# Score products of the recurrent heads: the second head of each pair in the other half of TensorE's columns

## The chip, the cores and the metric

The kernel runs on one core of one Trainium2 chip. The metric is the device time of one execution in microseconds (us); runs of the same kernel are summed up by their median. A profile of one execution gives the span from its first to its last instruction, and that is a little shorter than the time of a run.

The engines are named as in the profile: PE is TensorE's matrix multiply, PEld its loading of the stationary operand ("weights", here also keys), DVE is VectorE, ACT is ScalarE, POOL is GpSimd and SP is SyncE. Matmuls write into PSUM; only PE writes there by multiplying, and ACT and DVE read from there. A PSUM tile here has 128 partitions of 512 float32 values.

## The reference, cut to what matters

The reference is a trunk of two layers over 512 frames of 1024 channels. Each layer has a feed-forward block, a mixing block, a cross-attention into 256 memory tokens and a second feed-forward block. The change is in the mixing block, in the part with four recurrent heads of 128 channels:

```python
proj = h @ w_in[l]
q_a, f_a, i_a, g_a, u_b = jnp.split(proj, splits, axis=-1)
...
log_f = jnp.logaddexp(jnp.log(lbh), jnp.log1p(-lbh) + jax.nn.log_sigmoid(z))
k = (1.0 - lbh) * jax.nn.sigmoid(-z)
...
b = jnp.cumsum(gc, axis=2)
o_inter = jnp.einsum('bhtk,bhkv->bhtv', qc * jnp.exp(b), S)
rel = b[:, :, :, None, :] - b[:, :, None, :, :]
decay = jnp.exp(jnp.where(causal, rel, -jnp.inf))
A = jnp.einsum('bhtk,bhsk,bhtsk->bhts', qc, kc, decay)
o = o_inter + jnp.einsum('bhts,bhsv->bhtv', A, vc)
```

So each head needs, in each stretch of frames, a triangle of scores A[t, s]: query t times key s, with every channel decayed by the product of the forget gates between s and t.

## The kernel before, in words

The frames lie along the free axis: a head's `q`, `f` (forget gate), `kg` (key) are 128 channels by 512 frames. Heads go in pairs: `g` is the pair (0 or 1), `hh` the head in it. The 512 frames are NT = 4 blocks of P = 128 frames, HT = 256 is half of the frames.

The kernel works the triangle of a 128-frame block out by levels, `levels()` in `mix` (L809): m = 1, 2, 4, ... 64. At level m the block is cut into pieces of 2m frames; queries of a piece's second half meet keys of its first half. Between levels, keys (`kg`, L849) and queries (`qf`, L850) are multiplied by the forget products `tot` of the half that lies between them, so no exponent is ever needed. All scores end in `atd`, one 128 by 128 tile (key by query) for every head and block, which is read as an operand at L974.

Level 1 is done by column sums. Levels 2 to 32 are `dense(g, m)` (L785). `first_halves` (L767) has gathered the keys of all first halves, 64 a block, into `keys`. For each head and block a float32 matmul multiplies 64 keys by 64 queries (L793): eight matmuls a pair, which write partitions 0 to 63 of one PSUM tile, one head in columns 0 to 255, the other in 256 to 511. Only small squares on the diagonal of each 64 by 64 result are wanted. At level 32 they are copied from PSUM to `atd` by four small ACT copies a pair (L798). At levels 2 to 16 ACT copies each pair's tile into one half of `packed` (L802), and after the second pair ACT issues DMAs that bring the rows of `packed` to the partitions of `spread` at which those keys stand in `atd` (L807): 2, 4, 8 and 4 DMAs at levels 2, 4, 8 and 16. One level later DVE copies them into `atd` under a mask (`place`, L763). Level 64 (L824 to L833) has its own matmuls (L831) and one ACT copy a pair (L832).

What sets the order: the levels are a generator that is stepped between other matrix products of the stage (gate columns, value rows, pooling columns) at places written out by hand, `STEPS`. Each engine runs its own instructions strictly in the order the program has for it, and a scheduler at build time may bring other ready work forward. Tiles of PSUM used here come from one pool of four, `ps_tile`. ACT's queue carries its copies, the casts of weights (`split`, L76: `whi`; DVE makes `wlo` at L77) and the issue of the `spread` DMAs, all in one order. Weights are split five blocks ahead of their use and loaded seven ahead, by SP's queue.

Of the kernel before, what the change touches and what calls it, by code (L numbers as in the profile page):

```python
# [7 lines left out]
F32 = mybir.dt.float32  # L8
# [6 lines left out]
P = 128  # L15
D = 1024
T = 512
# [3 lines left out]
NT = T // P  # L21
# [25 lines left out]
def trunk_kernel(ctx: ExitStack, tc: tile.TileContext, ap: dict, out: bass.AP):  # L47
    nc = tc.nc
    pe, act, dve, pool = nc.tensor, nc.scalar, nc.vector, nc.gpsimd
# [11 lines left out]
    def ps_tile():  # L61
        return pp.tile([P, 512], F32, tag="ps", name="ps")
# [5 lines left out]
    def s_tile(shape, dt, name):  # L68
        return sp.tile(shape, dt, tag="s", name=name)
# [401 lines left out]
    HT = T // 2  # L471
# [242 lines left out]
    def mix(l, norm, mem, after):  # L714
# [4 lines left out]
        atd = [s_tile([P, 2, NT, P], F32, "atd") for _ in range(2)]  # L719
# [3 lines left out]
        for h in range(H):  # L723
            ps = ps_tile()
# [12 lines left out]
        for h in range(H):  # L737
            ps = ps_tile()
# [6 lines left out]
        def products(a, b):  # L745

            t = tp.tile([P, T], F32, tag="sq", name="qk", bufs=4)
            hl = s_tile([P, 2, T], F32R, "qkp")
            pool.tensor_tensor(t if len(a.shape) == 2 else t.rearrange("p (h n) -> p h n", h=2), a, b, op=ALU.mult)
            split(hl[:, 0], hl[:, 1], t)  # L750
            return hl

        def column_sums(ps, hl):

            for c in range(2):
                pe.matmul(ps, ones_r, hl[:, c], start=c == 0, stop=c == 1)  # L756

        def place(g, m, rows):

            o = atd[g].rearrange("p h i (b e j) -> p (h i) b e j", e=2, j=m)[:, :, :, 1, :]  # L760
            src = rows.rearrange("p (x b j) -> p x b j", x=2 * NT, j=m)
            mk = masks[m].rearrange("p (o b j) -> p o b j", o=1, j=m).broadcast_to([P, 2 * NT, 64 // m, m])
            dve.copy_predicated(o, mk, src)  # L763

        keys = [None, None]

        def first_halves(g, m):  # L767


            keys[g] = tp.tile([P, T], F32, tag="sq", name="keys", bufs=4)  # L770
            src = kg[g].rearrange("p h (b e j) -> p h b e j", e=2, j=m)[:, :, :, 0, :]
            if m > 4:
                act.copy(keys[g].rearrange("p (h b j) -> p h b j", h=2, j=m), src)
                return
            for hh in range(2):
                dst = keys[g][:, hh * HT:(hh + 1) * HT].rearrange("p (i j b) -> p i b j", i=NT, j=m)
                act.copy(dst, src[:, hh].rearrange("p (i b) j -> p i b j", i=NT))
# [4 lines left out]
        spread = {m: spreads[i % 2] for i, m in enumerate((2, 4, 8, 16))}  # L782
        packed = [None]

        def dense(g, m):  # L785


            ps = ps_tile()
            for hh in range(2):
                for i in range(NT):  # L790
                    c = hh * HT + i * 64
                    b = qf[g][:, hh, i * P:(i + 1) * P].rearrange("p (b e j) -> p b e j", e=2, j=m)[:, :, 1, :]
                    pe.matmul(ps[0:64, c:c + 64], keys[g][:, c:c + 64], b, start=True, stop=True)  # L793
            if m == 32:
                for b in range(2):
                    src = ps[b * 32:b * 32 + 32].rearrange("p (h i t) -> p h i t", h=2, i=NT)[:, :, :, b * 32:b * 32 + 32]
                    for hh in range(2):
                        act.copy(atd[g][b * 64:b * 64 + 32, hh, :, b * 64 + 32:b * 64 + 64], src[:, hh])  # L798
                return
            if g == 0:  # L800
                packed[0] = s_tile([64, 2, T], F32, "packed")
            act.copy(packed[0][:, g], ps[0:64])  # L802
            if g == 1:
                n = max(m, 64 // m)
                for x in range(64 // n):
                    rows = slice(x, P, 2 * m) if m <= 4 else slice(2 * m * x, 2 * m * x + m)
                    nc.scalar.dma_start(spread[m][rows], packed[0][x * n:(x + 1) * n])  # L807

        def levels():  # L809

            tot = f
            odd = [qf[g].rearrange("p h (n e) -> p h n e", e=2)[:, :, :, 1] for g in range(2)]
            even = [kg[g].rearrange("p h (n e) -> p h n e", e=2)[:, :, :, 0] for g in range(2)]
            near = [[products(q[g][:, hh], kg[g][:, hh]) for hh in range(2)] + [products(odd[g], even[g])] for g in range(2)]
            yield
            for m in (1, 2, 4, 8, 16, 32, 64):
                nb = T // (2 * m)
                tots = [None, None]  # L820
                if 1 < m <= 32:
                    for g in range(2):
                        dense(g, m)
                elif m > 32:  # L824
                    for g in range(2):
                        ps = ps_tile()
                        for hh in range(2):
                            for i in range(NT):
                                a = kg[g][:, hh, i * P:i * P + 64]
                                b = qf[g][:, hh, i * P + 64:(i + 1) * P]  # L830
                                pe.matmul(ps[0:64, (hh * NT + i) * 64:(hh * NT + i + 1) * 64], a, b, start=True, stop=True)  # L831
                        act.copy(atd[g][0:64, :, :, 64:128].rearrange("p h i t -> p (h i) t"),  # L832
                                 ps[0:64, :].rearrange("p (x t) -> p x t", t=64))  # L833
                for g in range(2):
                    if m == 1:
                        for hh in range(2):
                            ps = ps_tile()
                            column_sums(ps, near[g][hh])
                            dve.tensor_tensor(atd[g][:, hh], ps.rearrange("p (i t) -> p i t", t=P),
                                              ident.rearrange("p (o t) -> p o t", o=1).broadcast_to([P, NT, P]), op=ALU.mult)  # L840
                            yield
                        ps = ps_tile()
                        column_sums(ps, near[g][2])
                        place(g, m, ps)
                    tv = tot[g].rearrange("p h (b e) -> p h b e", e=2)
                    kv = kg[g].rearrange("p h (b e j) -> p (h b) e j", e=2, j=m)
                    qv = qf[g].rearrange("p h (b e j) -> p (h b) e j", e=2, j=m)
                    tx = tot[g].rearrange("p h (b e) -> p (h b) e", e=2)
                    dve.tensor_tensor(kv[:, :, 0, :], kv[:, :, 0, :], tx[:, :, 1:2].broadcast_to([P, 2 * nb, m]), op=ALU.mult)  # L849
                    dve.tensor_tensor(qv[:, :, 1, :], qv[:, :, 1, :], tx[:, :, 0:1].broadcast_to([P, 2 * nb, m]), op=ALU.mult)  # L850
                    nt_ = s_tile([P, 2, nb], F32, "tot") if m == 1 else sm.tile([P, 2, nb], F32, tag=f"tot{m}", name="tot", bufs=2)
                    dve.tensor_tensor(nt_, tv[:, :, :, 0], tv[:, :, :, 1], op=ALU.mult)
                    tots[g] = nt_
                    if m < 32:
                        first_halves(g, 2 * m)
                    if m == 1:
                        yield
                if 2 < m <= 32:
                    for g in range(2):
                        place(g, m // 2, spread[m // 2][:, g])  # L860
                if m > 1:
                    yield
                tot = tots
            last.extend(tot)
# [26 lines left out]
        def recurrent():  # L891
            yield from levels()
            turn(0), turn(1), turn(2)
            yield
# [14 lines left out]
        for h in range(H):  # L909
            ps = ps_tile()  # L910
# [7 lines left out]
        for k2 in range(NK // 2):  # L918
            wh, wl = wts.next()
            for e in range(2):  # L920
                k = 2 * k2 + e
                for i in range(NT):
                    sl = slice(i * P, (i + 1) * P)
                    mm3(accs[i], (norm.h[k][0][:, sl], norm.h[k][1][:, sl]), (wh[:, e], wl[:, e]),
                        start=k == 0, stop=k == NK - 1)
# [6 lines left out]
        for g in POOL_ORDER:  # L932
            win = 2 ** (g + 1)
            ps = ps_tile()
# [5 lines left out]
            src, dst, w_ = u, sa, 1  # L940
            while w_ < win:
                pool.tensor_tensor(dst[:, 16:], src[:, 16:], src[:, 16 - w_:16 + T - w_], op=ALU.add)
                src, dst = dst, (sb if dst is sa else sa)
# [23 lines left out]
        o = [None] * H  # L967
# [328 lines left out]
```

## Time and profile before

| | |
|---|---|
| runs | 2098.34, 2098.62, 2100.18 us |
| median of 3 | 2098.62 us |
| span of the profiled execution | 2096.8 us |
| mean granted TensorE clock | 0.999 of full speed |
| recurrent-score stage, layer 0 | about 400 to 490 us after the start |
| the same, layer 1 | about 1440 to 1530 us |

How to read the lines that follow. A page opens with the busy time of each engine, its share of the span and its number of instructions. The chain of work is followed back from the last instruction, at each step to what released it. A line of a timeline has the start in us, the duration in us, engine, source line, operation, output tile, inputs, shapes and a count of merged instructions, then the engine's idle time before it and what ended that. The view of one source line or tile lists minimum, median and maximum duration in ns. Instructions that issue DMAs stand under the queue of their engine (ACTq is ACT's) and aren't counted as busy. Some tile names: `whi` and `wlo` are the two parts of a split weight block, `h` the normed input, `sg` the gates.

### The profile page before, as it was taken

What the parts mean: (1) busy time and instruction counts of PE and PEld (TensorE: products, weight loads), DVE (VectorE), ACT (ScalarE), POOL (GpSimd) and SP (SyncE); (2) the same over time, 40 slices, a digit from 0 to 9 for tenths busy, and PEclk for the clock granted to TensorE, in tenths of its full rate; (3) what the DMA queues carried; (4) which work ended last, traced back from release to release, by engine and by line L of the source; (5) the groups of instructions that cost most, each with busy time, mean ns of one, the idle gap of its engine ahead of it and who ended that gap; (6) DMA issues with size and microseconds to landing.
All of it is one profiled execution on the core that took longest, in us unless ns stands there. A gap on an engine that the chain in (4) does not pass through costs nothing.

```text
span 2096.8 us, 29543 instructions
## 1 busy us (share of the span) xinstructions
PE 2087.3 (100%) x11538; PEld 1809.1 (86%) x11538; DVE 1412.3 (67%) x2126; ACT 919.8 (44%) x1465; POOL 205.0 (10%) x204
## 2 busy tenths in 40 slices
PE   9999999999999999999999999999999999999998
PEld 8889898888888888989888898988888888889897
DVE  7758576677646585766776685757776556768575
ACT  6425344434544343544534353445344444435343
POOL 1100000302000110000021000003210001100000
PEclk9999999999999999999999999999999999999999
DMA  5364554233533246646425746532334331474552
GB/s 187 119 182 124 145 156 161 61 99 98 151 103 103 61 131 171 157 122 185 123 69 153 188 116 177 158 108 71 92 112 135 111 112 45 141 208 124 146 138 79
DMA packets 107868, 268.33 MB, mean 128 GB/s; under 512 B 10832, under 2 KB 12880, under 8 KB 107728
## 3 DMA queue, kind: packets, MB, share of 16 engines
q1 hardware_dynamic: 93952, 224.49, 32.9%
q0 software_dynamic: 11952, 38.02, 10.3%
q10 hardware_dynamic: 1824, 3.93, 0.8%
q8 instruction: 91, 1.49, 0.3%
q14 instruction: 49, 0.40, 0.1%
HBM read 256.70 MB, written 2.10 MB: 123 GB/s over the span
## 4 chain that ended last, share of the span: by engine, by line
PE 98%; DVE 1%; issue 1%; ACT 0%; POOL 0%; POOLq 0%; ACTq 0%; DVEq 0%
PE ps L86 19%; PE ps L84 19%; PE ps L85 19%; PE acc L554 8%; PE acc L84 8%; PE acc L85 8%; PE acc L86 8%; PE acc L555 4%; PE ps L1025 1%; PE ps L793 1%; PE ps L1026 1%; PE ps L974 0%; PE ps L1091 0%; PE acc L346 0%; PE ps L756 0%
## 5 line engine op out<-in xcount | busy, mean ns | idle before, releaser
L77 DVE TENSOR_TENSOR wlo<-raw,whi 128x1024 fp32r<-128x1024 f32 (+1 forms) x334 | 394.5, 1202 | 78.4 <-ACT whi L76 63.2
L76 ACT CAST whi<-raw 128x1024 fp32r<-128x1024 f32 (+1 forms) x334 | 330.3, 1018 | 113.1 <-DMA raw<-in_ffn_w_dram 49.9
L85 PE MATMUL ps<-h,whi 128*128 128x512 f32 x848 | 330.2, 390 | 0.0
L84 PE MATMUL ps<-h,whi 128*128 128x512 f32 x848 | 329.7, 391 | 0.0
L86 PE MATMUL ps<-h,wlo 128*128 128x512 f32 x848 | 329.5, 390 | 0.0
L554 PE MATMUL acc<-bhl,whi 128*128 128x512 f32 x744 | 266.3, 398 | 0.0
L86 PE MATMUL ps<-bhl,wlo 128*128 128x256 f32 x744 | 210.8, 284 | 0.2
L85 PE MATMUL ps<-bhl,whi 128*128 128x256 f32 x744 | 209.9, 283 | 0.0
L84 PE MATMUL ps<-bhl,whi 128*128 128x256 f32 x744 | 209.8, 283 | 0.0
L555 PE MATMUL acc<-bhl,wlo 128*128 128x256 f32 x744 | 204.8, 281 | 0.0
L76 ACT CAST whi<-wsum 128x1024 fp32r<-128x1024 f32 x124 | 130.1, 1050 | 151.8 <-DVE wsum L165 87.3
L86 PEld LDWEIGHTS ps<-h,wlo 128*128 128x128 f32 x848 | 159.2, 188 | 33.4
L84 PEld LDWEIGHTS ps<-h,whi 128*128 128x128 f32 x848 | 159.1, 188 | 33.1
L85 PEld LDWEIGHTS ps<-h,whi 128*128 128x128 f32 x848 | 159.2, 188 | 32.9
L77 DVE TENSOR_TENSOR wlo<-wsum,whi 128x1024 fp32r<-128x1024 f32 x124 | 153.8, 1240 | 47.7 <-ACT whi L76 45.5
L554 PEld LDWEIGHTS acc<-bhl,whi 128*128 128x128 f32 x744 | 137.7, 189 | 24.0
L84 PEld LDWEIGHTS ps<-bhl,whi 128*128 128x128 f32 x744 | 141.6, 190 | 4.1
L86 PEld LDWEIGHTS ps<-bhl,wlo 128*128 128x128 f32 x744 | 141.5, 190 | 2.5 <-DVE wlo L77 1.6
L555 PEld LDWEIGHTS acc<-bhl,wlo 128*128 128x128 f32 x744 | 141.1, 190 | 2.8
L85 PEld LDWEIGHTS ps<-bhl,whi 128*128 128x128 f32 x744 | 141.6, 190 | 1.9
L134 POOL DMA_DIRECT2D wsum<-in_ffn_w_dram x62 | 53.9, 869 | 765.5 <-DMA wsum<-in_ffn_w_dram 364.5
L84 PE MATMUL acc<-ahl,whi 128*128 128x512 f32 x328 | 128.0, 390 | 0.0
(271 smaller groups left out, 4128.9 us busy)
## 6 DMA issues: line engine op xcount, KB each, us to landing
raw<-in_ffn_w_dram SPq DMA_DIRECT2D x198, 512.0 KB
wsum<-in_ffn_w_dram SPq DMA_DIRECT2D x124, 256.0 KB
wsum<-in_ffn_w_dram POOLq DMA_DIRECT2D x62, 512.0 KB, 6.8
raw<-in_w_in_dram SPq DMA_DIRECT2D x32, 512.0 KB
raw<-in_ffn_w_dram SPq DMA_DIRECT2D x62, 256.0 KB
raw<-in_w_out_dram SPq DMA_DIRECT2D x16, 512.0 KB
raw<-in_xa_wk_dram SPq DMA_DIRECT2D x16, 512.0 KB
raw<-in_xa_wq_dram SPq DMA_DIRECT2D x16, 512.0 KB
```

The source lines that it names most:

```text
L76: act.copy(hi, src)
L77: dve.tensor_tensor(lo, src, hi.bitcast(F32), op=ALU.subtract)
L84: pe.matmul(o, a[0], b[0], start=start, stop=False, skip_group_check=more)
L85: pe.matmul(o, a[0], b[1], start=False, stop=False, skip_group_check=more)
L86: pe.matmul(o, a[1], b[0], start=False, stop=stop, skip_group_check=more)
L134: nc.gpsimd.dma_start(s1, c2, accum_op=ALU.add)
L554: pe.matmul(ps.rearrange("p (c t) -> p c t", t=HT), w[0], t, start=start and k == 0, stop=False, skip_group_check=True)
L555: pe.matmul(ps[:, :HT], w[1], t[:, 0], start=False, stop=k == 3, skip_group_check=True)
L793: pe.matmul(ps[0:64, c:c + 64], keys[g][:, c:c + 64], b, start=True, stop=True)
L1025: pe.matmul(ps.rearrange("p (c m) -> p c m", m=M), whl[0][:, k], mn[k], start=k == 0, stop=False, skip_group_check=True)
L1026: pe.matmul(ps[:, :M], whl[1][:, k], mn[k][:, 0], start=False, stop=k == NK - 1, skip_group_check=True)
```

## The change

At levels 2 to 64 the second head of each pair writes partitions 64 to 127 of the PSUM tile, where the first head writes 0 to 63, and the loops are turned so that the two heads alternate, block by block. Each head then needs 256 columns of the tile, so at levels 2 to 32 both pairs share one tile. At levels 2 to 16 one ACT copy of 128 by 512 takes the place of two of 64 by 512; the rows of the two heads are now apart, so each DMA to `spread` becomes two of half the bytes. At level 32 the four copies a pair stay, with other source places, and at level 64 one copy a pair becomes two of half the length. Nothing else is changed.

```diff
         def dense(g, m):
-            ps = ps_tile()
-            for hh in range(2):
-                for i in range(NT):
+            if g == 0:
+                packed[0] = ps_tile()
+            ps = packed[0]
+            for i in range(NT):
+                for hh in range(2):
                     c = hh * HT + i * 64
                     b = qf[g][:, hh, i * P:(i + 1) * P].rearrange("p (b e j) -> p b e j", e=2, j=m)[:, :, 1, :]
-                    pe.matmul(ps[0:64, c:c + 64], keys[g][:, c:c + 64], b, start=True, stop=True)
+                    o = g * HT + i * 64
+                    pe.matmul(ps[hh * 64:hh * 64 + 64, o:o + 64], keys[g][:, c:c + 64], b, start=True, stop=True)
             if m == 32:
-                for b in range(2):
-                    src = ps[b * 32:b * 32 + 32].rearrange("p (h i t) -> p h i t", h=2, i=NT)[:, :, :, b * 32:b * 32 + 32]
-                    for hh in range(2):
-                        act.copy(atd[g][b * 64:b * 64 + 32, hh, :, b * 64 + 32:b * 64 + 64], src[:, hh])
+                for hh in range(2):
+                    for b in range(2):
+                        src = ps[hh * 64 + b * 32:hh * 64 + b * 32 + 32, g * HT:(g + 1) * HT]
+                        src = src.rearrange("p (i t) -> p i t", i=NT)[:, :, b * 32:b * 32 + 32]
+                        act.copy(atd[g][b * 64:b * 64 + 32, hh, :, b * 64 + 32:b * 64 + 64], src)
                 return
-            if g == 0:
-                packed[0] = s_tile([64, 2, T], F32, "packed")
-            act.copy(packed[0][:, g], ps[0:64])
             if g == 1:
+                t = s_tile([P, 2, HT], F32, "packed")
+                act.copy(t.rearrange("p g t -> p (g t)"), ps)
                 n = max(m, 64 // m)
                 for x in range(64 // n):
                     rows = slice(x, P, 2 * m) if m <= 4 else slice(2 * m * x, 2 * m * x + m)
-                    nc.scalar.dma_start(spread[m][rows], packed[0][x * n:(x + 1) * n])
+                    for hh in range(2):
+                        nc.scalar.dma_start(spread[m][rows, :, hh * HT:(hh + 1) * HT], t[hh * 64 + x * n:hh * 64 + (x + 1) * n])
...
                     for g in range(2):
                         ps = ps_tile()
-                        for hh in range(2):
-                            for i in range(NT):
+                        for i in range(NT):
+                            for hh in range(2):
                                 a = kg[g][:, hh, i * P:i * P + 64]
                                 b = qf[g][:, hh, i * P + 64:(i + 1) * P]
-                                pe.matmul(ps[0:64, (hh * NT + i) * 64:(hh * NT + i + 1) * 64], a, b, start=True, stop=True)
-                        act.copy(atd[g][0:64, :, :, 64:128].rearrange("p h i t -> p (h i) t"),
-                                 ps[0:64, :].rearrange("p (x t) -> p x t", t=64))
+                                pe.matmul(ps[hh * 64:hh * 64 + 64, i * 64:(i + 1) * 64], a, b, start=True, stop=True)
+                        for hh in range(2):
+                            act.copy(atd[g][0:64, hh, :, 64:128], ps[hh * 64:hh * 64 + 64, :HT].rearrange("p (i t) -> p i t", t=64))
```

## The prediction

> **What bounds the kernel now.** I read the page first: span, busy shares, chain.
>
> ```profile
> span 2096.8 us, 29543 instructions
> PE 2087.3 (100%) x11538; PEld 1809.1 (86%) x11538; DVE 1412.3 (67%) x2126; ACT 919.8 (44%) x1465; POOL 205.0 (10%) x204
> PE 98%; DVE 1%; issue 1%; ACT 0%; POOL 0%; POOLq 0%; ACTq 0%; DVEq 0%
> ```
>
> PE works without a break and 98% of the chain is PE. A microsecond taken from PE's own work is therefore worth a microsecond, as long as the next PE instruction finds its operands ready. ACT, at 44%, has room on average, but averages say nothing of the stage that is edited. So next come the instructions of the edited line (level 2 to 32 scores), and the timeline around one group of them.
>
> ```profile
> L793 PEld LDWEIGHTS ps<-qf,keys x320: 132/138/138, 425.9 to 1500.9; 128*64 128x64 f32 x160
> L793 PE MATMUL ps<-qf,keys x320: 218/222/271, 425.9 to 1500.9; 128*64 128x64 f32 x160
> L831 PE MATMUL ps<-qf,kg x64: 222/222/270, 469.0 to 1509.9; 128*64 128x64 f32 x64
> ```
>
> Each float32 matmul is two records, a load of 64 columns and a matmul each. 320 + 64 records are 12 groups of 32: six levels in two layers.
>
> ```profile
> 425.54 0.39 PE L86 MATMUL ps<-h,wlo 128*128 128x512 f32 x1
> 425.85 1.94 PEld L793 LDWEIGHTS ps<-qf,keys 128*64 128x64 f32 x32 [0.35 <-issue]
> 425.85 2.08 PE L793 MATMUL ps<-qf,keys 128*64 128x64 f32 x32
> 427.86 0.50 PE L84 MATMUL ps<-h,whi 128*128 128x512 f32 x1
> 428.20 0.39 PE L85 MATMUL ps<-h,whi 128*128 128x512 f32 x1
> ```
>
> The group starts at 425.85 and hands over at 427.86: 2.01 us of PE. From first to last load start it is 1.94 - 0.138 = 1.80 us over 31 steps, 58 ns a record. What paces a record? Two rows of other small matmuls help.
>
> ```profile
> 366.07 0.95 PE L346 MATMUL acc<-ones,sq 128*128 128x1 f32 x8
> 366.07 0.86 PEld L346 LDWEIGHTS acc<-ones,sq 128*128 128x128 f32 x7
> 483.84 0.72 PE L884 MATMUL ps<-v,kt 128*128 128x128 f32 x5
> L884 PE MATMUL ps<-v,kt x48: 270/275/347, 483.1 to 1530.1; 128*128 128x128 f32 x48
> L84 PEld LDWEIGHTS ps<-h,whi 128*128 128x128 f32 x848 | 159.1, 188 | 33.1
> ```
>
> The first two rows belong to matmuls that stream one single column behind a load of 128 columns. Loads of that shape last 0.188 us (last row), so their step is (0.86 - 0.19)/6 = 112 ns. In the third row 128 columns are streamed behind the same size of load, and the step is (0.72 - 0.275)/4 = 111 ns, with 0.275 us for one (fourth row). One column or 128, the step is the same, so the load sets it: 112 ns for 128 columns, and 58 ns, about half, for our 64. All twelve groups together are 12 x 32 x 0.058 = 22.3 us, which is all that the edit can work on.
>
> **The change part by part.**
>
> *PE order and columns.* The instruction count stays: 32 records a group, of the same shapes. The second head's products now end in partitions 64 to 127, that is in the other 64 columns of the array, and the two heads alternate. If a load for one half can run while the other half loads or multiplies, two records fit in 58 ns and a group falls by 16 x 0.058 = 0.93 us, all groups by 11.1 us. If loads still go one behind the other, the gain is 0. No group of before uses columns 64 to 127, so the trace can't choose. A loss on PE itself is excluded: no record is added, and the 128*64 form, with the 0.2 to 0.3 us it costs to enter and leave, is there already. I take the full 11.1, because the "128*64" form already shows the array cut in two with one half idle, and because the load row of 58 ns says that loads scale with columns.
>
> The Trainium skill, "TensorEngine Tiling (Array Packing)", Key Properties, says that different tiles can load weights and multiply in parallel; that gives the 11.1. Against the change stands the Trainium skill, "TensorE: Matmul & The Clock Gate", The mechanism (Part 3): loads overlap running matmuls only if their row groups differ. Here both heads use all rows, and the sum by that rule would be 0; but the trace already has loads of all rows under matmuls of all rows (86% PEld beside 100% PE), so it bears the rule out poorly.
>
> *ACT: one copy instead of two (levels 2 to 16), twice the DMAs.*
>
> ```profile
> L807 ACTq DMA_DIRECT2D spread<-packed x36: 518/626/1212, 429.6 to 1494.6; - x36
> 444.43 0.58 ACT L802 COPY packed<-ps 64x512 f32<-64x512 f32 x1 [6.39 <-PE ps L793]
> 446.99 6.25 ACTq L807 DMA_DIRECT2D spread<-packed  x8
> 453.28 1.06 ACT L802 COPY packed<-ps 64x512 f32<-64x512 f32 x2 [5.80 <-DMA spread<-packed]
> 454.37 3.00 ACTq L807 DMA_DIRECT2D spread<-packed  x4
> 457.42 1.05 ACT L76 CAST whi<-raw 128x1024 fp32r<-128x1024 f32 x1 [3.08 <-DMA spread<-packed]
> 459.45 1.05 ACT L76 CAST whi<-raw 128x1024 fp32r<-128x1024 f32 x1 [0.98 <-DVE atd L763]
> 461.14 1.77 ACT L798 COPY atd<-ps 32x128 f32<-32x128 f32 x8 [0.64 <-PE ps L793]
> ```
>
> Levels 2, 4, 8, 16 issue 2, 4, 8, 4 DMAs a layer, 18, and now 36. At 0.626 us that is 18 x 0.626 = 11.3 us more of ACT's queue a layer, against four copies of some 0.5 us saved. Queued behind it are level 16's copy (which already waited 5.80 us), the weight casts, and the copies of level 32. The casts have cover: 457.42 is the first block of the output projection, whose first matmul is in the last fence below at 490.15, over 30 us later. The level 64 copies become two of half the length for one, off the path. A move of the DMA bytes costs nothing: they are the same. The issue run of level 8 ends at 446.99 + 6.25 = 453.24; with 8 x 0.626 = 5.0 more and one copy less, about 4.5 us later. Who waits is DVE:
>
> ```profile
> 458.08 1.33 DVE L763 COPY_PREDICATED atd<-fixed,spread 128x512 f32<-128x512 int32 x2 [3.40 <-DMA spread<-packed]
> 464.77 0.68 DVE L850 TENSOR_TENSOR qf<-qf,tot 128x512 f32<-128x512 f32 x1
> 459.95 2.08 PE L793 MATMUL ps<-qf,keys 128*64 128x64 f32 x32
> 461.96 0.50 PE L84 MATMUL ps<-h,whi 128*128 128x512 f32 x1
> 468.99 2.08 PE L831 MATMUL ps<-qf,kg 128*64 128x64 f32 x32
> 1501.73 0.68 DVE L850 TENSOR_TENSOR qf<-qf,tot 128x512 f32<-128x512 f32 x1
> 1508.09 2.08 PE L831 MATMUL ps<-qf,kg 128*64 128x64 f32 x32
> ```
>
> DVE already idles 3.40 us for level 8's DMAs in layer 0; behind that wait stand the v scalings, two weight splits, and the level 32 product qf, which level 64's matmuls read. That product ends at 465.45 and is read at 468.99: slack 3.5 us; in layer 1 it is 1508.09 - 1502.41 = 5.7 us. With PE faster, three groups put the DMAs 3 x 0.93 = 2.8 us earlier, so DVE is 4.5 - 2.8 = 1.7 us late, while PE comes to level 64 some 5 x 0.93 - 1.1 = 3.5 us early (the 1.1 is the next charge). Loss in layer 0: 1.7 + 3.5 - 3.5 = 1.7 us; in layer 1: 1.7 + 3.5 - 5.7, below 0, none.
>
> *Level 32 in one PSUM tile.* Both pairs now share one tile, and ACT copies out the first pair's scores while the second pair's matmuls write its other half. If the program orders these, the second half of the group waits for four copies: in before the group runs from 459.95, its second half from 461.0; ACT's eight copies start at 461.14 and take 1.77, four some 0.9, so PE would go on at 462.1: 1.1 us a layer, 2.2 in all. If not ordered, 0; if ACT comes late, more (the third rival). I take 2.2. The Trainium skill, "PSUM — Partial Sum Buffer", PSUM bank collisions raise a hardware error, has two engines' accesses to one bank and quadrant kept apart by the scheduler, which makes this wait likely; no run here shows it yet.
>
> *Tail of the stage.* Once levels end, PE waits a little on DVE:
>
> ```profile
> 485.46 0.55 PE L874 MATMUL ps<-fixed,kg 128*128 128x128 f32 x3 [0.21 <-DVE u L939]
> 486.19 0.91 PE L884 MATMUL ps<-v,kt 128*128 128x128 f32 x6 [0.18 <-DVE st L888]
> 488.25 0.71 PE L974 MATMUL ps<-v,atd 128*128 128x128 f32 x4 [0.38 <-DVE st L888]
> 490.15 0.39 PE L84 MATMUL acc<-h,whi 128*128 128x512 f32 x1
> ```
>
> These 0.77 us grow when PE is early and DVE is not: I put 0.6 us a layer, 1.2, an estimate from these rows.
>
> **Sum.** 2096.8 - 11.1 + 1.7 + 2.2 + 1.2 = 2090.8 us of span. The median of the runs, 2098.6, is 1.8 above the profiled span, so the forecast is 2092.6. About 0.2%, 4.2 us, is what a measurement of this kernel can tell from no change.
>
> **Rivals.**
>
> *A, the forecast (chance 0.5):* the halves run side by side. Its own range goes from the whole gain without a charge, 2098.6 - 11.1 = 2087.5, to half the gain with all charges, 2098.6 - 5.6 + 5.1 = 2098.1.
>
> *B, no change (0.3):* loads go one at a time, so 58 ns a record stays and nothing that the edit says about columns shortens PE. For it: the step follows the load alone in both rows of 128 columns. Against: those rows load one and the same column range each time. The Trainium skill's rule of row groups, named above, would end here. Then the charges are 2.2 at level 32, and at level 64 DVE's 4.5 less the slack of 3.5, 1.0 in layer 0: 2098.6 + 3.2 = 2101.8.
>
> *C, slower (0.2):* the level 32 hold becomes long. ACT is one queue: level 8's and 16's issue runs end (8 + 4) x 0.626 = 7.5 us later, less two saved copies, 6.5: at 457.4 + 6.5 = 463.9. Then two casts of 1.05 and four copies of 0.9 in sum follow: 466.9. The second half of level 32's group, due at 461.0, is held 5.9 us a layer, 11.8 in all. It decides if PE's order puts these 16 records right behind the first 16 rather than behind a weight block. For it: the added DMAs sit on just this queue. Against: after 461.96 PE has ready weight-block matmuls that could be put between. With half of the gain it gives 2098.6 - 5.6 + 11.8 = 2104.8; with none, 2110.4. It makes the change slower once the hold is over (4.2 + 5.6)/2 = 4.9 us a layer.
>
> **Chances.** A is faster by over 0.2% in 0.42 of its 0.5, within in 0.08. B is within in 0.26, slower in 0.04. C is slower in 0.18 and within in 0.02. Faster 0.42, within 0.36, slower 0.22. The range takes A's lower end, 2087.5, and C with half of the gain, 2104.8, and leaves out about the worse half of C and a little below A.
>
> **What would show it.** In the after profile, the row of a 32-record group: 1.0 to 1.1 us from its start to the next block if A holds, 2.0 if B. Loads of the two halves should overlap in PEld. Twice the DMA issues at the new line, level 8's run near 10 to 11 us. DVE's idle time for spread in layer 0 above 3.40. At level 32 either two groups of 16 with other matmuls between (cheap) or idle PE time released by ACT's copies (C). Wrong would be: PE groups shortened in full and the time unmoved, or idle PE time at a place not named here.

## The result, and the profile after

The changed kernel takes 2109.87 us, the median of five runs (2108.63 to 2111.01), against 2098.62 for the kernel before: a ratio of 1.0053, 95% interval 1.0041 to 1.0064. It is slower, by 11 us. The profiled span is 2108.2 us.

First the page of the changed kernel.

```profile
span 2108.2 us, 29590 instructions
PE 2081.0 (99%) x11538; PEld 1802.7 (86%) x11538; DVE 1409.0 (67%) x2126; ACT 917.3 (44%) x1461; POOL 211.1 (10%) x204
```

PE is busy 6 us less than before in a span that is 11 us longer. So the matmuls did get cheaper, and somewhere PE stood still. The timeline shows both. One group of 32 records at level 2:

```profile
425.73 1.02 PEld L796 LDWEIGHTS ps<-qf,keys 128*64 128x64 f32 x32 [0.35 <-issue]
425.73 1.16 PE L796 MATMUL ps<-qf,keys 128*64 128x64 f32 x32
426.82 0.50 PE L84 MATMUL ps<-h,whi 128*128 128x512 f32 x1
```

From the group's start to the next block it is 1.09 us where it was 2.01, with the same 32 loads and 32 matmuls: two records start about every 58 ns, one in each half. Twelve groups give 12 x 0.92 = 11 us, all that was forecast. Now PE's rows from level 32 on, with the matmuls of the weight blocks left out:

```profile
456.14 0.69 PE L796 MATMUL ps<-qf,keys 128*64 128x64 f32 x16
...
463.78 0.69 PE L835 MATMUL ps<-qf,kg 128*64 128x64 f32 x16
464.30 0.64 PE L796 MATMUL ps<-qf,keys 128*64 128x64 f32 x16
474.14 1.12 PE L835 MATMUL ps<-qf,kg 128*64 128x64 f32 x16 [9.20 <-DVE qf L854]
...
1518.28 1.13 PE L835 MATMUL ps<-qf,kg 128*64 128x64 f32 x16 [9.05 <-DVE qf L854]
```

Level 32 (L796) is split. Its second pair comes 8 us after its first, and only behind the first pair of level 64 (L835). Then PE idles for 9.20 us until DVE has made that pair's `qf`. Layer 1 has the same wait, 9.05 us (last row). Why is level 32 split? ACT's timeline:

```profile
443.16 1.28 ACTq L811 DMA_DIRECT2D spread<-packed  x1
...
444.48 11.39 ACTq L811 DMA_DIRECT2D spread<-packed  x15
455.91 0.59 ACT L806 COPY packed<-ps 128x512 f32<-128x512 f32 x1 [11.32 <-DMA spread<-packed]
456.39 1.05 ACT L76 CAST whi<-raw 128x1024 fp32r<-128x1024 f32 x1
456.52 5.22 ACTq L811 DMA_DIRECT2D spread<-packed  x8
461.84 1.06 ACT L802 COPY atd<-ps 32x128 f32<-32x128 f32 x4 [4.40 <-DVE u L943]
```

The first pair's scores of level 32 are in PSUM at about 456.9, and ACT copies them out at 461.84, behind level 8's and level 16's issues, which end at 456.52 + 5.22 = 461.74. (The row names a product of DVE, the semaphore that came last by the profile, and that one ends at about the same time. In the kernel with two tiles, below, the copies again start 0.1 us behind the last issue, and another product of DVE is named.) The second pair's writes into the shared tile come only after these copies; with a tile of its own, below, the pair isn't held. PE had weight-block matmuls to do meanwhile, so it lost nothing there. The bill comes from DVE:

```profile
458.13 1.32 DVE L763 COPY_PREDICATED atd<-fixed,spread 128x512 f32<-128x512 int32 x2 [5.21 <-DMA spread<-packed]
...
460.48 0.69 DVE L854 TENSOR_TENSOR qf<-qf,tot 128x512 f32<-128x512 f32 x1
461.08 0.69 DVE L943 TENSOR_TENSOR u<-ps,rrow 128x512 f32<-128x512 f32 x1
465.08 1.58 DVE L763 COPY_PREDICATED atd<-fixed,spread 128x512 f32<-128x512 int32 x1 [3.31 <-ACT whi L76]
466.58 1.21 DVE L77 TENSOR_TENSOR wlo<-raw,whi 128x1024 fp32r<-128x1024 f32 x1
467.72 0.68 DVE L943 TENSOR_TENSOR u<-ps,rrow 128x512 f32<-128x512 f32 x1
468.32 0.67 DVE L853 TENSOR_TENSOR kg<-kg,tot 128x512 f32<-128x512 f32 x1
468.92 1.52 DVE L854 TENSOR_TENSOR qf<-qf,tot 128x512 f32<-128x512 f32 x1
470.36 2.28 DVE L77 TENSOR_TENSOR wlo<-raw,whi 128x1024 fp32r<-128x1024 f32 x1
472.56 1.52 DVE L854 TENSOR_TENSOR qf<-qf,tot 128x512 f32<-128x512 f32 x1
```

In the kernel before, the two level 32 products `qf` stood 1.2 us apart, 464.77 being the second, and this the first:

```profile
463.55 0.69 DVE L850 TENSOR_TENSOR qf<-qf,tot 128x512 f32<-128x512 f32 x1
```

Here the first is at 460.48 and the second at 472.56, although its matmuls were done at 464.9. The program has put it behind other DVE work, among it two weight splits, which are made five blocks ahead of their use, and DVE itself ran late: it waited 5.21 us for level 8's `spread` and 3.31 us before level 16's, whose issues ACT ended at 461.74 (the row names the last semaphore, which is ACT's). PE's next instruction needs that product.

Part of the 9.20 us is DVE running long. While POOL works,

```profile
468.54 1.35 POOL L946 TENSOR_TENSOR sa<-u 128x512 f32<-128x512 f32 x1 [2.43 <-DVE u L943]
469.85 3.69 POOL L946 TENSOR_TENSOR sb<-sa 128x512 f32<-128x512 f32 x2
```

the two products `qf` take 1.52 us each and a split 2.28, where the same shapes take 0.69 and 1.21 in other rows of DVE above: 2.7 us more in front of PE's next matmul. The trace shows the two together; that POOL is the cause wasn't tried.

The idle time has a tail. Two stretches behind it, with their length, the busy time and count of PE, PEld, DVE, ACT and POOL, the granted clock, the DMA share and GB/s; and two 512-column matmuls in a row:

```profile
474.10:480.00 5.90, 5.86 (x28) 4.76 (x29) 5.36 (x10) 1.78 (x3) 1.71 (x5) 0.54 0.29 87
480.00:486.00 6.00, 6.00 (x32) 4.99 (x31) 1.29 (x2) 1.49 (x3) 2.21 (x3) 1.00 0.23 85
477.07 0.63 PE L85 MATMUL ps<-h,whi 128*128 128x512 f32 x1
477.50 0.63 PE L86 MATMUL ps<-h,wlo 128*128 128x512 f32 x1
```

Over the 5.9 us behind the wait the granted clock is 0.54 on average, and matmuls that normally follow each other by 0.23 us do so by 0.43. That costs another 2.5 us a layer. The sum: -11.0 for the groups, +9.2 and +9.05 for the two waits, +5 for the slow clock, -0.8 for the small waits at the stage's end that went: 2096.8 + 11.4 = 2108.2, and the span is 2108.2.

### The profile page after: what moved, and what is told of

The parts are those of the page before. It is cut to its first block, busy times and chain, and to the rows that moved or that the text cites. A ratio compares the mean times of both kernels' runs of the same rounds, so it can differ in the third digit from the quotient of the medians.

```text
span 2108.2 us, 29590 instructions
## 1 busy us (share of the span) xinstructions
PE 2081.0 (99%) x11538; PEld 1802.7 (86%) x11538; DVE 1409.0 (67%) x2126; ACT 917.3 (44%) x1461; POOL 211.1 (10%) x204
## 3 DMA queue, kind: packets, MB, share of 16 engines
q8 instruction: 91, 1.49, 0.3%
```

## The experiments

Theory 1 blames the shared tile at level 32 alone, theory 2 the doubled DMA issues alone, theory 3 both together. Two edits, each undone alone and both together, tell them apart; a fourth kernel adds only the DMAs to the kernel before. All four ran on one chip, with the kernel before at 2098.77 us.

**A tile for each pair at level 32, 36 DMAs a layer.**

```diff
-            if g == 0:
+            if g == 0 or m == 32:
                 packed[0] = ps_tile()
```

> The changed kernel, but at level 32 each pair has a PSUM tile of its own; doubled DMAs stay. Theory 1 (the shared tile at level 32 holds the second pair back behind ACT's copies, and that wait alone makes the 9.2 us of idle PE in each layer): the idle time goes, the 10 groups' gain of about 0.95 us each and level 64's stay, ratio to before about 0.995, 2088 us. Theory 2 (the doubled DMA issues delay ACT and through it DVE, whatever the tiles): the idle time stays near 9 us a layer, ratio about 1.005. Theory 3 (it takes both): a wait of 2 to 4 us a layer, ratio 0.997 to 1.000.

Measured: 2095.40 us, ratio 0.9985 (0.9976 to 0.9993). PE and ACT:

```profile
456.32 1.15 PE L796 MATMUL ps<-qf,keys 128*64 128x64 f32 x32
464.43 1.15 PE L835 MATMUL ps<-qf,kg 128*64 128x64 f32 x32
478.04 0.55 PE L878 MATMUL ps<-fixed,kg 128*128 128x128 f32 x3 [2.23 <-DVE u L943]
```

```profile
461.96 2.15 ACT L802 COPY atd<-ps 32x128 f32<-32x128 f32 x8 [4.34 <-DVE qf L854]
```

ACT is as late as in the changed kernel (461.96), but level 32 is whole again and level 64 waits for nobody. What is left of the lateness shows at the stage's end, where PE waits 2.23 us for DVE; that is the longest of four such waits, 5.3 us in the two layers. Theory 2 alone falls; the gain isn't all back, so theory 1 alone falls as well.

**The 18 DMAs of before, tile still shared.**

```diff
-                t = s_tile([P, 2, HT], F32, "packed")
-                act.copy(t.rearrange("p g t -> p (g t)"), ps)
+                t = s_tile([64, 2, T], F32, "packed")
+                for hh in range(2):
+                    act.copy(t[:, :, hh * HT:(hh + 1) * HT], ps[hh * 64:hh * 64 + 64].rearrange("p (g t) -> p g t", g=2))
...
-                    for hh in range(2):
-                        nc.scalar.dma_start(spread[m][rows, :, hh * HT:(hh + 1) * HT], t[hh * 64 + x * n:hh * 64 + (x + 1) * n])
+                    nc.scalar.dma_start(spread[m][rows], t[x * n:(x + 1) * n])
```

> The changed kernel, but at levels 2 to 16 two ACT copies of 64 by 512 bring the two heads' rows together again, so that the DMAs are the 18 a layer of before; the shared tile at level 32 stays. Theory 1 (shared tile alone): level 64's second half still waits, 5 to 9 us a layer, ratio 1.000 to 1.005. Theory 2 (DMA issues alone): ratio about 0.995, 2088 us. Theory 3 (both): 2 to 4 us a layer, ratio 0.997 to 1.000.

Measured: 2091.01 us, ratio 0.9963 (0.9949 to 0.9976). ACT and PE:

```profile
456.94 1.06 ACT L802 COPY atd<-ps 32x128 f32<-32x128 f32 x4
```

```profile
455.97 0.69 PE L796 MATMUL ps<-qf,keys 128*64 128x64 f32 x16
462.02 0.69 PE L796 MATMUL ps<-qf,keys 128*64 128x64 f32 x16
464.45 1.15 PE L835 MATMUL ps<-qf,kg 128*64 128x64 f32 x32
```

The shared tile still splits level 32, but ACT copies as soon as the scores are there, 456.94, and the second pair goes at 462.02, ahead of level 64 as it should. No PE wait follows at level 64. The split itself is nearly free. The 2 to 4 us a layer that theory 3 gave here didn't come; the time lies nearer to theory 2's. With the run before, this means that each repair alone takes the wait at level 64 away.

**Both repairs** (the two diffs above together).

> Both repairs: a tile for each pair at level 32 and the 18 DMAs of before, with the two heads still in the two column halves in turns. All three theories expect no idle PE of over 0.5 us at level 64 and the full gain of about 11 us: ratio about 0.995, 2088 us. If it stays above 2094, something else in the change costs time.

Measured: 2090.79 us, ratio 0.9962 (0.9949 to 0.9974). So with 18 DMAs the shared tile costs 2091.01 - 2090.79 = 0.2 us, and with 36 it costs 2109.87 - 2095.40 = 14.5 us; the DMAs cost 4.6 us with tiles of their own and 18.9 with the shared one (2109.87 - 2091.01). Neither fault alone makes the result: theory 3, and by more than the sum of the two. The full 11 us aren't reached; 8.0 are:

```profile
481.08 0.50 PE L84 MATMUL ps<-pthl,pw 128*128 128x512 f32 x1 [2.07 <-DVE u L943]
```

PE, which now comes earlier to the stage's end, waits there for DVE, which had waited 0.93 us for POOL. PE's waits of this kind are 3.7 us in the two layers, where the kernel before had 0.8.

**Only the DMAs doubled, in the kernel before.**

```diff
-                    nc.scalar.dma_start(spread[m][rows], packed[0][x * n:(x + 1) * n])
+                    for hh in range(2):
+                        cs = slice(hh * HT, (hh + 1) * HT)
+                        nc.scalar.dma_start(spread[m][rows, :, cs], packed[0][x * n:(x + 1) * n, :, cs])
```

> The kernel before, with nothing changed but each DMA to spread cut in two by heads (36 a layer). Theory 1: ACT and DVE wait longer but PE has its order and its slack of 3.5 and 5.7 us, ratio 1.000 to 1.001. Theory 2: the PE wait at level 64 shows here too, several us a layer, ratio 1.003 or more. Theory 3: up to 1 us a layer, ratio 1.000 to 1.001.

Measured: 2104.45 us, ratio 1.0026 (1.0016 to 1.0036). The issues, DVE's wait for `spread` in all (us, times), and the largest PE wait:

```profile
L809 ACTq DMA_DIRECT2D spread<-packed x72: 598/645/1285, 429.4 to 1506.6; - x72
...
  DVE atd L763: 29.9, 8
```

```profile
482.42 0.55 PE L876 MATMUL ps<-fixed,kg 128*128 128x128 f32 x3 [1.10 <-DVE u L941]
```

DMAs of half the size take as long to issue as whole ones (0.645 us). The cost, 5.7 us, is more than theories 1 and 3 gave, and PE doesn't wait at level 64, where theory 2 had it. Most of it is at the stage's end again, in several waits: with the longest, 1.10 us, they add up to 4.7 us in the two layers, where the kernel before had 0.8. The rest isn't placed.

The next three ran together, with the kernel before at 2098.86 us.

**Second head's DMAs issued by SP,** the changed kernel otherwise.

```diff
-                        nc.scalar.dma_start(...)
+                        (nc.sync if hh else nc.scalar).dma_start(...)
```

> The changed kernel as it is (shared tile, 36 DMAs a layer), but the second head's DMAs are issued from SP's queue, so that ACT issues 18 as before. Theory 'ACT's queue': what costs is the time that issues take in ACT's order; the 9 us of idle PE at level 64 go and the time is near that of the kernel with 18 DMAs, 2091 to 2094 us. Rival 'number of DMAs': their landing comes late whoever issues them, or SP issues them late behind weight loads; DVE still waits, idle PE at level 64 stays at several us a layer, 2100 us or more.

Measured: 2095.71 us, ratio 0.9984 (0.9976 to 0.9993).

```profile
468.26 0.69 PE L835 MATMUL ps<-qf,kg 128*64 128x64 f32 x16 [2.70 <-DVE qf L854]
...
469.45 0.63 PE L85 MATMUL ps<-h,whi 128*128 128x512 f32 x1
```

The count of DMAs is the same, only ACT's share is halved, and 14.2 us of the time go. So the issue time in ACT's order is the larger part. A wait of 2.70 us at level 64 stays, and slow matmuls behind it (0.63 us for 0.39): the theory's 2091 to 2094 was missed.

**Both repairs, loops not in turns.**

```diff
-            for i in range(NT):
-                for hh in range(2):
+            for hh in range(2):
+                for i in range(NT):
...
```

The loops of level 64 are turned in the same way.

> The kernel with both repairs (a tile a pair at level 32, 18 DMAs a layer), but the loops not turned: four products of the first head, then four of the second, still in the other column half. Theory 'turns': PE starts its instructions in order, so only neighbours in different halves run side by side; here one record in eight has such a neighbour, a group takes about 1.7 to 1.9 us instead of 1.0, and the time is 2099 to 2101 us. Rival 'halves alone': the array picks later work of the idle half itself; groups stay at 1.0 us and the time at 2091 us.

Measured: 2094.59 us, ratio 0.9980 (0.9971 to 0.9989).

```profile
426.28 1.56 PE L796 MATMUL ps<-qf,keys 128*64 128x64 f32 x32
427.77 0.50 PE L84 MATMUL ps<-h,whi 128*128 128x512 f32 x1
```

A group takes 1.49 us: between the two answers, and below the 1.7 to 1.9 of the first. (1.56 - 0.22)/0.058 is 23 steps, where 32 records one by one take 31. The single loads of this group in the trace say where: they start 55 to 64 ns apart, but nine times two start within 3 ns of each other, three times at each of the three changes of head. A change offers one pair of neighbours in different halves. The first load of the second head starts at 291 ns, when two loads of the first head, at 346 and 404 ns, are still to come, if the program keeps the order of the loops, which the records don't name. So records of the idle half start ahead of their turn, but not far enough to make the turns useless, which are worth 0.4 us a group here.

**Both repairs, every second DMA from SP** (the same edit by `x % 2`).

> The kernel with both repairs, with every second one of its 18 DMAs a layer issued from SP's queue, so ACT issues 9. If ACT's issue run of 6 us at level 8 still costs the repaired kernel something (DVE waits for spread there, and PE waits 2 to 3 us at the stage's end), the time falls from 2090.8 to 2088 us or so. If that end wait is the chain of DVE and POOL after the last level, it stays at 2090 to 2091 us. If SP brings the DMAs late behind its weight loads, it is slower, 2092 us or more.

Measured: 2089.48 us, ratio 0.9956 (0.9942 to 0.9969): 1.3 us below the kernel with both repairs, whose interval overlaps this one. The time lies between the first two answers. PE's waits for DVE at the stage's end are 2.5 us in the two layers, against 3.7 with both repairs alone; that fits a small part of them being ACT's issue run, which the times alone don't show.

The last two ran with the kernel before at 2099.26 us.

**Level 32's copies by DVE,** the changed kernel otherwise.

```diff
-                        act.copy(atd[g][b * 64:b * 64 + 32, hh, :, b * 64 + 32:b * 64 + 64], src)
+                        dve.tensor_copy(atd[g][b * 64:b * 64 + 32, hh, :, b * 64 + 32:b * 64 + 64], src)
```

> The changed kernel as it is (shared tile, 36 DMAs a layer from ACT), but the eight level 32 copies a layer are made by DVE, not ACT. Theory 'place in ACT's queue': the second pair was held because ACT reads the shared tile only after its 24 DMA issues of levels 8 and 16 (copies at 461.8 us, 5 us after the first pair's matmuls). DVE reads it sooner, level 32's second half goes ahead of level 64 again, the 9.2 us idle falls below 1 us, and the time is near that with two tiles, 2093 to 2097 us. Rival 'any reader of a shared tile': the hold moves to DVE, which itself waits for spread until 458 us, and idle PE of 4 to 9 us a layer stays: 2102 to 2110 us.

Measured: 2104.86 us, ratio 1.0025 (1.0016 to 1.0034). DVE and PE:

```profile
458.59 1.32 DVE L763 COPY_PREDICATED atd<-fixed,spread 128x512 f32<-128x512 int32 x2 [4.71 <-DMA spread<-packed]
...
461.54 1.18 DVE L802 COPY atd<-ps 32x128 f32<-32x128 f32 x4
...
470.94 1.31 DVE L854 TENSOR_TENSOR qf<-qf,tot 128x512 f32<-128x512 f32 x1
```

```profile
472.31 1.12 PE L835 MATMUL ps<-qf,kg 128*64 128x64 f32 x16 [6.83 <-DVE qf L854]
```

The narrow theory falls: away from ACT's queue, the copies come no earlier (461.54), since DVE stands waiting for the same late `spread` DMAs. The rival holds: any reader that the DMAs delay holds the second pair.

**Both repairs, all 18 DMAs from SP** (the same edit, without a choice).

> The kernel with both repairs, with all 18 DMAs a layer issued from SP's queue and none from ACT's. If issue time on ACT is what is still dear, it is a little faster than with half of them there (2089.5 us), 2088 to 2089 us. If SP's own run of issues, in one order with the weight loads, takes ACT's place as the late queue, 2090 to 2093 us.

Measured: 2089.42 us, ratio 0.9954 (0.9941 to 0.9966): the same as with half of them there, and between the two answers. What remains of the end wait, 0.94 us in layer 0 where it was 2.07, isn't ACT's:

```profile
479.98 0.50 PE L84 MATMUL ps<-pthl,pw 128*128 128x512 f32 x1 [0.94 <-DVE u L943]
```

This kernel and the one with every second DMA from SP have the lowest medians of the study, 9 to 10 us under the kernel before.

## Why the prediction was wrong

The forecast was 2092.6 us, with a range of 2087.5 to 2104.8; the changed kernel took 2109.87.

*Columns side by side: right, in size too.* 0.93 us a group was forecast, 0.92 measured. Of the two rules of the Trainium skill weighed there, "TensorEngine Tiling (Array Packing)", Key Properties, is borne out: loads and matmuls of the halves run in parallel. The Trainium skill's rule from "TensorE: Matmul & The Clock Gate", The mechanism (Part 3), that loads overlap matmuls only across row groups, isn't: 32 loads of all rows fit in 1.02 us. Rival B is out.

*Doubled DMAs: mechanism right, too small.* The prediction had level 8's run at 10 to 11 us and level 16's to follow; it was 12.7 (443.16 to 455.87) and 5.2. It took 0.626 us an issue, the median of all, for issues that come in runs; its own row of eight issues in 6.25 us has 0.78 each, and twice that run is 12.5. It charged 1.7 at level 64 and 1.2 at the end, 2.9 in all; alone the DMAs cost 4.6 to 5.7, most of it in waits at the end of the stage, where the prediction thought of the small waits of before and not of DVE's whole backlog. The 1.7 at level 64 shows in neither kernel that has the DMAs alone.

*Level 32 in one tile: the step that failed.* It was charged as a length, 1.1 us a layer, for PE standing still between two halves of the group. PE didn't stand still there. The hold changed the order: the second pair went behind level 64's first pair, and its `qf` behind the rest of DVE's work. The wait appeared one level later, as 9.2 us and a slow clock. The prediction even named "two groups of 16 with other matmuls between" as the cheap outcome. It is cheap with ACT on time and dear with ACT late, by the two runs with a shared tile: 0.2 against 14.5 us.

*Rival C* had the right pair of causes, ACT's issue runs and the shared tile, and the sign. It had the place wrong (level 32 instead of level 64), and its price of 5.9 us a layer stands against a wait of 9.1 us and 2.5 us of slow clock. It got a chance of 0.2 because ready weight-block matmuls were counted against it: they covered the hold, but not what the hold did to the order.

*Terms that were summed apart belong together.* The forecast added 1.7, 2.2 and 1.2; the runs show that the first makes the second.

What stays open: why the scheduler at build time put the second pair's `qf` so far back in DVE's order wasn't tried; only that it does so in the three kernels with the shared tile and 36 DMAs. Part of DVE's lateness before that is the landing of DMAs, part their issue; the run with SP's queue bounds the issue part from below but doesn't split it fully.

## What to carry to other kernels

Packing two 64-column products into the two halves of the array, in turns, halves their time, if the outputs can leave PSUM without more DMAs: a second copy with shifted partitions was cheaper than twice the DMAs. When two producers share one PSUM tile, count not the wait for its reader but what is ordered behind the second producer, on every engine. A DMA issue costs the issuing queue the same for half the bytes, so count issues in the order of that engine, not bytes.

## What the runs showed of the hardware

Loads are paced by half: with both halves in use 32 loads of 64 columns take 1.02 us, against 1.94 with one. Without turns, nine pairs of loads started together where the order of the loops offers three pairs of neighbours, so PE can start records of the other half before earlier ones of the first (if the program keeps that order).

After an idle PE stretch of 9.2 us the granted clock was 0.54 over 5.9 us, and after one of 2.7 us six 512-column matmuls also took 0.63 instead of 0.39 us. With both repairs the clock was 0.50 from 483 to 485 us, shortly after a wait of 2.07 us; with two tiles it stayed at 1.00 behind a wait of 2.23 us in layer 0. So the length of one wait doesn't decide it alone. The Trainium skill, "TensorE: Matmul & The Clock Gate", Part 1, has the clock halved once a window of about 3.4 us was idle; the long wait agrees with it, the waits of 2.7 and 2.07 us show that less can be enough.

The issue of a `spread` DMA from ACT had nearly the same median whole and cut in half, 0.626 and 0.645 us, in kernels that differ in nothing else.
